# Seams between the stages of an encoder block: a wider first group, other block sizes, u copied in portions, squares summed by TensorE

## The chip, the core and the metric

The kernel runs on one core of one Trainium2 chip. A core has TensorE (PE; its weight loads are PEld), VectorE (DVE), ScalarE (ACT), GpSimd (POOL) and SyncE (SP, which here only issues DMAs). The metric is the device time of one execution in microseconds (us), as the median of several runs. 512 frames of 1024 channels go through one layer.

## What is computed

The reference, cut to what matters (all in float32):

```python
mod = (silu(c) @ w_ada + b_ada).reshape(B, 3, 3, 1024)
h = modulate(rms_norm(x, g_ffn1), mod[:, 0, 0], mod[:, 0, 1])
x = x + 0.5 * mod[:, 0, 2] * swiglu(h, w_ffn1_in, w_ffn1_out)

h = modulate(rms_norm(x, g_mix), mod[:, 1, 0], mod[:, 1, 1])
u_pool, u_ssm, gl_pool, gl_ssm = split(h @ w_in)
y_pool = multiscale_pool(u_pool, pool_w, pool_b, pool_scale) @ w_pool_up
y_ssm = s5_mixer(u_ssm, ...) @ w_ssm_up
x = x + mod[:, 1, 2] * ((sigmoid(gl_pool) * y_pool + sigmoid(gl_ssm) * y_ssm) @ w_out)

h = modulate(rms_norm(x, g_ffn2), mod[:, 2, 0], mod[:, 2, 1])
x = x + 0.5 * mod[:, 2, 2] * swiglu(h, w_ffn2_in, w_ffn2_out)
return rms_norm(x, g_final)
```

`swiglu` is `(silu(h @ Wa) * (h @ Wb)) @ Wout` with 2816 = 22 x 128 inner channels; a "tile" f below is one of these 22. The S5 mixer needs small tables (angles, powers, sines) that are computed from parameters.

## The kernel before, in words

**Arithmetic.** Frames lie along the free dimension, 128 channels on the partitions. A product is exact enough in three matmuls (`mm3`, L255-L258): every weight tile `raw` is split into a high part `wh` (a cast by ScalarE, L1295) and a low part `wl = raw - wh` (L1297, VectorE, or GpSimd if the unit has `pool_lo`); activations are split likewise into HH and HL, or GHA and GLA (`put_split`, L260-L262; `gslots` also has a slot pair in GC).

**Units.** The program is a list `units`, walked once in order. A unit with weights has its raw tile loaded by a DMA and split some units ahead (`split_at`, `load_at`, L1261-L1270: about two units of lead for the split, three buffers), then issues its matmuls (`mm`) and what follows from them (`post`). All engines take their instructions strictly in the order written. So an instruction of VectorE that waits holds up the splits written behind it, and through them TensorE.

**First feed-forward.** `group6` (L271) runs over the 8 chunks k of the input channels: per k it makes h (L215, L219, L246) and 18 matmuls of 512 columns for six output halves at once (three tiles f, with a and b). In this first group VectorE also computes the modulation `mod`: each k needs two dots of 1024 columns (L132), whose weights come by DMA. Then each further tile takes two in-units of 24 matmuls (ab = 0, 1), after the second of which `gate_store` (L399) forms silu(a) * b. After the tiles of a block (BLOCKS, L19: 6, 6, 5, 5 tiles) 8 out-units, one for each output chunk d, of 3 matmuls per tile, add to the residual (`residual`, L646). The unit loop's end (L1374-L1385) gives VectorE further work by the unit's index: one more dot from unit 16 on (`ada_step`), and from 18 on up to ten small operations for the SSM tables (`fill`, L707 in the profile).

**Seams.** The last two output chunks of each stage are done in `tail` (L330) by halves of the frames, HA and HB, so that the sum of squares of the next norm can start: squares by ScalarE (L185, L348), added into ACC by GpSimd (L186) or VectorE (L349), summed over the channels by TensorE with a column of ones (`norm_sum`, L192), then a root, a reciprocal and a matmul that spreads it over the partitions (`norm_rows`, L206).

**Mixer.** A `group6`, then 18 units of 24 matmuls for u, the gates and the rest. The group's four tiles of u_ssm are copied from PSUM to U in 16 pieces of 32 x 128 each (`ssm_u`, L992), before TensorE's `ssm_in` can use them; VectorE then does pool sums (L1075-L1085), complex products (L705) and scans (L1026).

**Second feed-forward.** `ffn_seven` (L447) computes the tiles 4 to 21 in pairs with seven products in the place of eight, in halves of 256 frames (`half_units`, matmuls at L492). Their operands are sums of h (`h_sums`, GpSimd, from float32 copies HF that GpSimd makes at L221) and of weights (GpSimd, L510-L512), split late (`late_splits`). The end is a tail, and eight products of `final` (L660) with their output DMAs.

## Time and profile before

| | |
|---|---|
| median of 3 runs | 1063.01 us (1061.71 to 1063.97) |
| the profiled execution | 1061.94 us, its span 1059.9 us |
| TensorE busy | 1025.5 us (97%) |
| VectorE busy | 750.5 us (71%) |
| ScalarE, GpSimd busy | 377.6, 405.7 us |
| HBM read | 134 MB, 130 GB/s over the span |

TensorE is nearly always busy, so its idle time, some 34 us, and the parts of the span where its granted clock (PEclk) is under 1.00 are all that another order could win. In the profile's rows an entry "[3.23 <-DVE wl L1297]" says that the engine sat idle for 3.23 us before the instruction until VectorE had written wl at line 1297. Names without a number are buffers; "x32" is a count. A row of a window gives, for each engine, busy time and instructions, then PEclk, the DMA engines' share and GB/s.

### The profile page before, as it was taken

To read this page: it belongs to the slowest core of one execution; us is meant where nothing else is said; L and a number is where in the kernel's file an instruction comes from. 1 tells how busy PE (TensorE), PEld (TensorE's weight loads), DVE (VectorE), ACT (ScalarE), POOL (GpSimd) and SP (SyncE) were. 2 spreads that over 40 slices of the span, in tenths; PEclk is the share of its full clock that TensorE was granted. 3 is DMA by queue.
4 is the path that set the end of the run, shared out by engine and by line. 5 is a ranking of instruction groups with operands and counts; after the bars stand their busy time and mean duration, and the time that the engine had idled before them with its cause. 6 is when DMAs were issued, how large, how long until landed. Compare 5 with 4: busy or idle time off the path is not lost.

```text
span 1059.9 us, 14235 instructions
## 1 busy us (share of the span) xinstructions
PE 1025.5 (97%) x5474; PEld 870.2 (82%) x5474; DVE 750.5 (71%) x1152; ACT 377.6 (36%) x546; POOL 405.7 (38%) x339
## 2 busy tenths in 40 slices
PE   7899999999999999989999999999999999999996
PEld 6678888888888888877888888887888998999895
DVE  6966888999796546689922365377984995798454
ACT  5242222222232243453243333235442442343244
POOL 2310200389885513044600000298762571475003
PEclk8999999999999999999999999999999999999998
DMA  9555555464566122412234223231351242235102
GB/s 347 213 198 181 198 200 189 171 227 166 176 243 219 58 76 76 130 40 90 92 102 145 80 100 100 60 117 63 100 179 40 100 157 63 80 106 173 61 20 80
DMA packets 45893, 138.22 MB, mean 130 GB/s; under 512 B 5105, under 2 KB 9329, under 8 KB 45826
## 3 DMA queue, kind: packets, MB, share of 16 engines
q1 hardware_dynamic: 45650, 136.73, 38.1%
q8 instruction: 43, 0.70, 0.3%
q0 software_dynamic: 176, 0.59, 0.1%
q14 instruction: 24, 0.20, 0.1%
HBM read 134.15 MB, written 3.15 MB: 130 GB/s over the span
## 4 chain that ended last, share of the span: by engine, by line
PE 82%; DVE 11%; POOL 2%; issue 1%; ACT 1%; DMA 1%; SPq 0%; DVEq 0%; ACTq 0%; POOLq 0%
PE ps L256 20%; PE ps L258 20%; PE ps L257 20%; PE ps L492 16%; PE ps L281 1%; PE ps L282 1%; DVE ev L705 1%; PE ps L285 1%; DVE U L997 1%; DVE ev L215 1%; DVE QM L132 1%; DVE TB L132 1%; DVE ACC L349 1%; DVE wl L1297 1%; PE ps L942 1%
## 5 line engine op out<-in xcount | busy, mean ns | idle before, releaser
L1297 DVE TENSOR_TENSOR wl<-raw,wh 128x1024 fp32r<-128x1024 f32 (+3 forms) x150 | 186.0, 1244 | 78.3 <-ACT wh L1295 78.1
L1295 ACT CAST wh<-raw 128x1024 fp32r<-128x1024 f32 (+3 forms) x164 | 150.4, 922 | 185.5 <-PE ps L257 99.9
L258 PE MATMUL ps<-HH,wl 128*128 128x512 f32 (+1 forms) x544 | 212.0, 390 | 4.6 <-DVE wl L1297 4.6
L256 PE MATMUL ps<-HH,wh 128*128 128x512 f32 (+1 forms) x544 | 212.6, 391 | 0.0
L257 PE MATMUL ps<-HL,wh 128*128 128x512 f32 (+1 forms) x544 | 211.7, 389 | 0.0
L258 PEld LDWEIGHTS ps<-HH,wl 128*128 128x128 f32 x544 | 102.3, 188 | 29.0 <-DVE wl L1297 5.4
L256 PEld LDWEIGHTS ps<-HH,wh 128*128 128x128 f32 x544 | 102.4, 188 | 23.4 <-ACT PM L938 0.2
L257 PEld LDWEIGHTS ps<-HL,wh 128*128 128x128 f32 x544 | 102.5, 188 | 23.3
L256 PE MATMUL ps<-GHA,wh 128*128 128x512 f32 (+1 forms) x308 | 118.8, 386 | 0.0
L258 PE MATMUL ps<-GHA,wl 128*128 128x512 f32 (+1 forms) x308 | 118.0, 383 | 0.0
L257 PE MATMUL ps<-GLA,wh 128*128 128x512 f32 (+1 forms) x308 | 117.9, 383 | 0.0
L186 POOL TENSOR_TENSOR ACC<-ACC,ev 128x512 f32<-128x512 f32 x15 | 19.4, 1296 | 246.8 <-ACT ev L185 246.7
L646 DVE SCALAR_TENSOR_TENSOR X<-ps,MOD,X 128x512 f32<-128x512 f32 (+1 forms) x78 | 55.0, 706 | 73.9 <-PE ps L258 73.9
L132 DVE CUSTOM_DVE_ANT_0 ADA<-ADA,C,COL 128x1024 f32<-128x1024 f32 x50 | 74.8, 1496 | 0.0
L256 PEld LDWEIGHTS ps<-GHA,wh 128*128 128x128 f32 x308 | 57.8, 188 | 12.7 <-ACT PM L938 0.4
L258 PEld LDWEIGHTS ps<-GHA,wl 128*128 128x128 f32 x308 | 57.8, 188 | 12.7
L257 PEld LDWEIGHTS ps<-GLA,wh 128*128 128x128 f32 x308 | 57.8, 188 | 12.3
L281 PE MATMUL ps<-HH,wh 128*128 128x512 f32 (+1 forms) x180 | 61.6, 358 | 6.0 <-ACT HH L219 5.9
L492 PE MATMUL ps<-SH,wl 128*128 128x256 f32 x216 | 61.0, 282 | 0.0
L282 PE MATMUL ps<-HH,wl 128*128 128x512 f32 (+1 forms) x180 | 60.3, 350 | 0.5 <-DVE wl L1297 0.5
L492 PE MATMUL ps<-SL,wh 128*128 128x256 f32 x216 | 60.7, 281 | 0.0
L492 PE MATMUL ps<-SH,wh 128*128 128x256 f32 x216 | 60.7, 281 | 0.0
(253 smaller groups left out, 2158.1 us busy)
## 6 DMA issues: line engine op xcount, KB each, us to landing
ADA<-w_ada SPq DMA_DIRECT2D x50, 512.0 KB, 3.6
raw<-w_f_in SPq DMA_DIRECT2D x40, 512.0 KB, 4.6
raw<-w_f_out SPq DMA_DIRECT2D x40, 384.0 KB, 4.1
raw<-w_in SPq DMA_DIRECT2D x18, 512.0 KB, 3.5
MISC<-w_f_in SPq DMA_DIRECT2D x18, 512.0 KB, 3.5
raw<-w_f SPq DMA_DIRECT2D x16, 384.0 KB, 3.9
raw<-w_f_out SPq DMA_DIRECT2D x16, 320.0 KB, 3.0
MM<-w_f_in SPq DMA_DIRECT2D x9, 512.0 KB, 3.6
```

The lines of the kernel that those rows point to most:

```text
L132: V.tensor_tensor_reduce(out=t, in0=t, in1=C, scale=1.0, scalar=bada[:, n:n + 1], op0=ALU.mult, op1=ALU.add, accum_out=MOD[:, n:n + 1],)
L186: eng.tensor_tensor(out=acc[:, cs], in0=acc[:, cs], in1=sq[:, cs], op=ALU.add)
L215: V.scalar_tensor_tensor(out=t[:, cs], in0=X[:, k, cs], scalar=GS[:, s * 8 + k:s * 8 + k + 1], in1=r[:, cs], op0=ALU.mult, op1=ALU.mult,)
L256: E.matmul(pst, wh, xh, start=first, stop=False)
L257: E.matmul(pst, wh, xl, start=False, stop=False)
L258: E.matmul(pst, wl, xh, start=False, stop=last)
L281: E.matmul(pst[m][:, cs], hi[:, w], xh, start=first, stop=False)
L282: E.matmul(pst[m][:, cs], lo[:, w], xh, start=False, stop=False)
L492: E.matmul(out_, w_[:, i, w], x_, start=first and n == 0, stop=last and n == 2, skip_group_check=True)
L646: V.scalar_tensor_tensor(out=X[:, d, cs], in0=p[:, cs], scalar=MOD[:, s * 24 + 16 + d:s * 24 + 17 + d], in1=X[:, d, cs], op0=ALU.mult, op1 ...
L1295: S.copy(out=hi[:, 0:u.cols], in_=t)
L1297: eng.tensor_tensor(out=lo[:, 0:u.cols], in0=t, in1=hi[:, 0:u.cols].bitcast(F32), op=ALU.subtract)
```

## The change

It has six parts.

1. The first feed-forward's group takes seven halves per k (three tiles and the a-half of a fourth; 896 columns), and the in-unit of that half goes. The low parts there are made by VectorE, each one unit ahead, and by GpSimd no longer; the first loads of weights are issued together. GpSimd's first instruction is now the load of the SSM tables.
2. BLOCKS becomes 5, 5, 6, 6. With the missing unit, the unit's index at which dots and small operations are handed out meets other units.
3. At the seams the last squares are not added by VectorE. `norm_sum` runs over several terms and lets TensorE add them. `prefetch` (splits and loads) comes later in the tail of stages 0 and 1, and at stages 1 and 2 the group's first two low parts are VectorE's, the third GpSimd's.
4. The four tiles of u are copied after the group, after each of the two u-units, and after the first gate unit (`gp`, m = 6). Within a tile the copying engine changes with t, not with m.
5. In the second feed-forward ScalarE makes the copies HF. After tile 3 come eight out-units of 4 tiles, the first four with one late split each, and then the pairs, with out-units of 6 tiles behind every third pair; a slot is found by `slot_of`. The last block has 6 tiles.
6. At the end GpSimd does one of the four last products of `final`.

```diff
-BLOCKS = ((0, 6), (6, 12), (12, 17), (17, 22))
+BLOCKS = ((0, 5), (5, 10), (10, 16), (16, 22))
...
-    def norm_sum(pc, cs=ALL):
+    def norm_sum(pc, cs=ALL, more=()):
...
-        for b in range(b0, b1):
-            E.matmul(pc[:, b:b + 1], ACC[:, b * P:(b + 1) * P], ONE[:, 0:1], start=True, stop=True)
+        terms = [ACC] + list(more)
+        for n, x in enumerate(terms):
+            for b in range(b0, b1):
+                E.matmul(pc[:, b:b + 1], x[:, b * P:(b + 1) * P], ONE[:, 0:1], start=n == 0 and b == b0,
+                         stop=n == len(terms) - 1, skip_group_check=True)
...
         if s == 2:
-            G.tensor_scalar(out=HF[k % 4][:, cs], in0=t[:, cs], scalar1=shift_col(s, k), scalar2=None, op0=ALU.add)
+            S.activation(out=HF[k % 4][:, cs], in_=t[:, cs], func=AF.Identity, bias=shift_col(s, k))
...
-            u = Unit(src[k], 768, mm, pre, (lambda: post(pst)) if k == KT - 1 else None)
-            u.pool_lo = pre0 is not None or k < 3
+            u = Unit(src[k], nm * P, mm, pre, (lambda: post(pst)) if k == KT - 1 else None)
+            u.pool_lo = pre0 is None and k == 2
...
-            rc = norm_sum(nrm["pc"], HA)
-            add6 = first(6, p6, HB)
+            rc = norm_sum(nrm["pc"], HA, [sq7])
+            sq6 = first(6, p6, HB)
...
-            prefetch()
-            add7 = first(7, p7, HB)
-            add6()
-            add7()
+            nrm["sq"] = [sq6, first(7, p7, HB)]
             if s < 2:
+                prefetch()
                 make_h(s + 1, 1, nrm["A"])
             else:
-                rc = norm_sum(nrm["pc"], HB)
+                rc = norm_sum(nrm["pc"], HB, nrm["sq"])
...
-                if m % 2:
+                if t % 2:
                     V.tensor_copy(out=o, in_=i)
                 else:
                     S.copy(out=o, in_=i)
...
-            for m in range(4):
-                ssm_u(m, pst[m])
+            held.extend(pst[0:4])
+            ssm_u(0, held[0])
...
+            return std_unit(wi[m], HH, HL, 8, lambda h: (pool_in(1 - m, h[0]), ssm_u(1 + m, held[1 + m])))
...
+                if m == 6:
+                    ssm_u(3, held[3])
...
+        n = len(units)
+        out_units(0, 4)
+        for u in units[n:n + 4]:
+            u.pre = lambda: late_splits.pop(0)()
...
+            if i in (6, 12):
+                out_units(i - 2, i + 4)
...
+        if j < KT:
+            split_at[j] = j - 1
...
+    rb = ev()
+    S.copy(out=rb[:, HB], in_=nrm["B"][0][:, HB])
+    final(0, 2, (rb, HB), G)
+    for k in range(2, KT, 2):
```

What this does to the order of VectorE's instructions at three places. First, one k of the first group (PM, QM and TB hold weights of the dots). Before:

```order
L215 SCALAR_TENSOR_TENSOR ev<-X,GS,ps 128x512
L132 ISA QM,MOD<-QM,C,COL 128x1024
L132 ISA MOD 128x1
L141 SCALAR_TENSOR_TENSOR GS<-MOD,COL 128x1
L246 SCALAR_TENSOR_TENSOR HL<-ev,MOD,HH 128x512
L132 ISA QM,MOD<-QM,C,COL 128x1024
```

After (the lines have moved by 3):

```order
L218 SCALAR_TENSOR_TENSOR ev<-X,GS,ps 128x512
L132 ISA QM,MOD<-QM,C,COL 128x1024
L132 ISA MOD 128x1
L141 SCALAR_TENSOR_TENSOR GS<-MOD,COL 128x1
L249 SCALAR_TENSOR_TENSOR HL<-ev,MOD,HH 128x512
L132 ISA QM,MOD<-QM,C,COL 128x1024
L132 ISA MOD 128x1
L1309 TENSOR_TENSOR wl<-raw,wh 128x896
```

VectorE's split of the weights has come to the end of each k. Second, the small operations of unit 30 (PM holds the tables in the making). Before, in an in-unit of block 2, between the splits of two units of 1024 columns:

```order
L1297 TENSOR_TENSOR wl<-raw,wh 128x1024
L132 ISA ADA,MOD<-ADA,C,COL 128x1024
L132 ISA MOD 128x1
L707 TENSOR_TENSOR PM<-PM 128x112
L707 TENSOR_SCALAR PM<-PM 128x112
L707 SCALAR_TENSOR_TENSOR PM<-PM 128x112 x5
L707 TENSOR_SCALAR PM<-PM 128x112
L707 SCALAR_TENSOR_TENSOR PM<-PM 128x112 x2
L1297 TENSOR_TENSOR wl<-raw,wh 128x1024
```

After, in an out-unit of block 2 (640 columns):

```order
L1309 TENSOR_TENSOR wl<-raw,wh 128x640
L651 SCALAR_TENSOR_TENSOR X<-ps,MOD,X 128x512
L132 ISA ADA,MOD<-ADA,C,COL 128x1024
L132 ISA MOD 128x1
L712 TENSOR_TENSOR PM<-PM 128x112
L712 TENSOR_SCALAR PM<-PM 128x112
L712 SCALAR_TENSOR_TENSOR PM<-PM 128x112 x5
L712 TENSOR_SCALAR PM<-PM 128x112
L712 SCALAR_TENSOR_TENSOR PM<-PM 128x112 x2
L1309 TENSOR_TENSOR wl<-raw,wh 128x640
```

The same ten operations now stand between the splits of shorter units, with a residual beside them. Third, VectorE's copies of u behind the mixer's group, with buffer numbers and the engines waited for. Before:

```order
L1085 TENSOR_TENSOR MISC_87<-MISC_87,FIX_93 128x4x4 [waits DMASW1_49,DVE_49]
L997 COPY U_3519<-ps_3203 32x128 [waits PE_49]
L997 COPY U_3519<-ps_3203 32x128 x15
L997 COPY U_3519<-ps_3205 32x128 [waits PE_49]
L997 COPY U_3519<-ps_3205 32x128 x15
L1297 TENSOR_TENSOR wl_3612<-raw_3475,wh_3611 128x1024 [waits DMAHW3_49,Activation_49]
```

After:

```order
L1090 TENSOR_TENSOR MISC_87<-MISC_87,FIX_93 128x4x4 [waits DMASW1_49,DVE_49]
L1002 COPY U_3522<-ps_3201 32x128 [waits PE_49,Activation_49]
L1002 COPY U_3522<-ps_3201 32x128 [waits Activation_49] x7
L1309 TENSOR_TENSOR wl_3567<-raw_3478,wh_3566 128x1024 [waits DMAHW2_49,Activation_49]
L1002 COPY U_3522<-ps_3202 32x128 [waits PE_49,Activation_49]
L1002 COPY U_3522<-ps_3202 32x128 [waits Activation_49] x7
```

There are eight copies of a tile on VectorE, not sixteen of two tiles, a split stands between two portions, and each copy waits for ScalarE; ScalarE's copies wait for VectorE in the same way.

## The prediction

> **What bounds the kernel now.** I read the page first, then the list of TensorE's waits, then the timelines of VectorE, ScalarE and TensorE at each of those waits, and windows of the stretches around them. The page says who is the bound:

> ```profile
> PE 1025.5 (97%) x5474; PEld 870.2 (82%) x5474; DVE 750.5 (71%) x1152; ACT 377.6 (36%) x546; POOL 405.7 (38%) x339
> ```

> TensorE is busy for 1025.5 of 1059.9 us, and the change leaves its large matmuls alone in number. So only TensorE's idle time and its low clock can be won, and any new wait of TensorE is lost in full. Where the idle time is, the waits of TensorE tell (columns: who waits for whom, us in total, times, longest):

> ```profile
> PE ps L281 <- ACT HH L219: 5.9, 7, 1.1
> PE ps L196 <- DVE ACC L349: 5.8, 5, 2.9
> PE ps L258 <- DVE wl L1297: 4.6, 2, 3.2
> PE ps L492 <- DVE wl L262: 3.1, 3, 1.4
> PE ps L206 <- DVE rc L200: 1.6, 2, 1.1
> PE ps L492 <- ACT wh L261: 1.3, 2, 1.1
> ```

> Every row is a seam: the first group (L281), the sums of squares between stages and at the end (L196, L206), the mixer's start (L258), the start of the second feed-forward's pair units (L492). The change works on all of these. VectorE has 29% of idle time overall, but it does not lie in the stretches where the change adds work, and that decides the sum.

> One pace is needed throughout. In the window 100 to 112 TensorE has no gap:

> ```profile
> 100.00:112.00 12.00, 12.00 (x53) 9.69 (x52) 8.54 (x16) 2.00 (x4) 0.00 (x0) 1.00 0.67 230
> ```

> Its 53 matmuls include some two cut by the edges, so a 512-column matmul takes about 0.233 us: a group unit of 6 tiles (18) 4.2, of 7 tiles (21) 4.9, an in-unit (24) 5.6, an out-unit of 5 tiles (15) 3.5.

> **The change part by part: the first group.** VectorE's and GpSimd's rows of one period:

> ```profile
> 28.01 0.74 DVE L215 SCALAR_TENSOR_TENSOR ev<-X,GS,ps 128x512 f32<-128x512 f32 x1
> 28.67 1.27 DVE L132 CUSTOM_DVE_ANT_0 QM<-QM,C,COL 128x1024 f32<-128x1024 f32 x1
> ...
> 30.06 0.74 DVE L246 SCALAR_TENSOR_TENSOR HL<-ev,MOD,HH 128x512 fp32r<-128x512 f32 x1
> 30.72 2.87 DVE L132 CUSTOM_DVE_ANT_0 QM<-QM,C,COL 128x1024 f32<-128x1024 f32 x1
> ...
> 33.53 0.73 DVE L215 SCALAR_TENSOR_TENSOR ev<-X,GS,ps 128x512 f32<-128x512 f32 x1
> ```
> ```profile
> 30.31 2.21 POOL L1297 TENSOR_TENSOR wl<-raw,wh 128x768 fp32r<-128x768 f32 x1 [3.31 <-ACT wh L1295]
> ```

> The split that VectorE does elsewhere, for 1024 and 768 columns:

> ```profile
> 178.88 1.22 DVE L1297 TENSOR_TENSOR wl<-raw,wh 128x1024 fp32r<-128x1024 f32 x1
> ...
> 201.12 0.95 DVE L1297 TENSOR_TENSOR wl<-raw,wh 128x768 fp32r<-128x768 f32 x1
> ```

> The period is 33.53 - 28.01 = 5.52 us against TensorE's 4.2, which makes the 1.1 us waits of L281. The second dot takes 2.87 instead of 1.27 because GpSimd's split runs beside it. After the change VectorE does the split itself: 5.52 - 1.60 + about 1.05 (896 columns, between 0.95 and 1.22) = 4.97, against 4.90 on TensorE for seven tiles. The group so takes the seventh tile, 24 x 0.233 = 5.6 us of later work, almost free: 7 periods of 5.52 become 7 of 4.97 (-3.9), the later unit goes (-5.6), the last run grows (+0.7), and unit 1 now waits for its split in VectorE's queue (+1 to +3). Sum -4.8, ends -3 and -7. GpSimd's queue now begins with the load of the SSM tables (576 KB), some 48 us earlier than now, amid the loads of the first tiles. I cost it at nothing, since the dots at 28.67 and 30.72 start with no idle time ahead, their tiles being there; uncovered it is rival four.

> **Blocks of 5, 5, 6, 6.** The small SSM operations are handed out ten to a unit, by the unit's index, whatever the unit's length. In before the heavy ones fall on in-units of 5.6 us. Now block 2's out-units, 3.5 us each, get them. The windows hold those of the units 29 to 34, VectorE's L707 only (length, busy):

> ```profile
> 176.85:178.90 2.05, 1.84 (x10) 1.00 0.44 140
> 181.27:184.00 2.73, 2.46 (x10) 1.00 0.56 183
> 188.32:190.93 2.61, 2.34 (x10) 1.00 0.52 165
> 193.02:195.30 2.28, 1.99 (x10) 1.00 0.48 156
> 199.36:201.15 1.79, 1.58 (x10) 1.00 0.46 98
> 203.90:205.53 1.63, 1.53 (x10) 1.00 0.37 68
> ```

> The other work of an out-unit on VectorE, and of the gate before it:

> ```profile
> 173.61 0.69 DVE L403 TENSOR_TENSOR ev<-ev,ps 128x512 f32<-128x512 f32 x1 [1.07 <-PE ps L258]
> 174.98 0.69 DVE L262 TENSOR_TENSOR GLA<-ev,GHA 128x512 fp32r<-128x512 f32 x1 [0.69 <-ACT GHA L261]
> ...
> 201.99 0.74 DVE L646 SCALAR_TENSOR_TENSOR X<-ps,MOD,X 128x512 f32<-128x512 f32 x1
> 202.65 1.27 DVE L132 CUSTOM_DVE_ANT_0 ADA<-ADA,C,COL 128x1024 f32<-128x1024 f32 x1
> ```

> From start to start a residual is 0.66 and a dot with its read 1.28; a split of 640 columns is about 0.74. So an out-unit holds VectorE for 0.74 + 0.66 + 1.28 = 2.7 plus its small operations of 2.0, 2.7, 2.6, 2.2, 1.7, 1.6: in sum 29.0 us, while TensorE needs 6 x 3.5 = 21.0. Count from the end of unit 28, where the gate (2.0, idle included), a dot and some 1.5 of small ones come first: the split for unit 31 is ready at 5.7, needed at 7.5; that for 32 at 10.4, needed at 11.0. Then splits are late: 33 by 1.4, 34 by 1.8, 35 by 1.4, 36 by 1.0, 37 by 1.2. That is 6.8 us of new waits, each too short to lower the clock; 0.2 more for a fuller stretch behind. **+7.0**, ends +4 (another unit of lead) and +9.

> **The seams of squares.** Behind the first feed-forward and the mixer the adds of L349 leave VectorE and TensorE sums the tiles itself. The rows for the end show the wait and what stands in it:

> ```profile
> 1045.93 0.58 PE L196 MATMUL ps<-ONE,ACC 128*128 128x1 f32 x4 [0.23 <-DVE ACC L349]
> 1051.34 0.61 PE L196 MATMUL ps<-ONE,ACC 128*128 128x1 f32 x4 [2.85 <-DVE ACC L349]
> ```
> ```profile
> 1049.55 1.73 DVE L349 TENSOR_TENSOR ACC<-ACC,ev 128x256 f32<-128x256 f32 x1 [0.21 <-ACT ev L348]
> ...
> 1053.76 2.48 DVE L663 TENSOR_TENSOR MISC<-X,ps 128x512 f32<-128x512 f32 x4 [1.32 <-PE ps L206]
> ```
> Of the 5.8 us in the list, 0.23 + 2.85 are these two; 2.7 are the inner seams, three waits of 0.9. They go, but each inner seam gets 6 more matmuls of one column. Two of them (four records) take 0.58, so one costs 0.2 to 0.3: 12 cost 2.4 to 3.6, of which two of a seam's six run while TensorE waits for the last square anyway. Net **-0.3 at each inner seam** (-1.3 to +0.5). At the end the first sum costs 0.2 more than its wait. The second then waits only for the last square, which is there when the add of it starts, at 1049.55: 1051.34 becomes 1049.6 (-1.7). Three finals instead of four stand on VectorE (2.48 / 4 = -0.6), and GpSimd does the fourth beside them. **-2.0** (-1 to -3).

> **The mixer's start.** The copies of u, all 32 x 128, and the waits behind them:

> ```profile
> 453.81 9.60 DVE L997 COPY U<-ps 32x128 f32<-32x128 f32 x32
> ...
> 463.44 1.23 DVE L1297 TENSOR_TENSOR wl<-raw,wh 128x1024 fp32r<-128x1024 f32 x1
> ```
> ```profile
> 448.80 8.63 ACT L999 COPY U<-ps 32x128 f32<-32x128 f32 x32
> ```
> ```profile
> 464.72 0.67 PE L258 MATMUL ps<-HH,wl 128*128 128x512 f32 x1 [3.23 <-DVE wl L1297]
> 496.64 0.50 PE L258 MATMUL ps<-HH,wl 128*128 128x512 f32 x1 [1.34 <-DVE wl L1297]
> ```
> ```profile
> 464.70:467.50 2.80, 2.78 (x7) 2.21 (x8) 1.86 (x3) 2.05 (x3) 0.00 (x0) 0.53 0.50 171
> 467.50:470.00 2.50, 2.50 (x11) 1.99 (x10) 2.14 (x6) 0.29 (x1) 0.00 (x0) 0.84 0.32 104
> ```

> In before ScalarE copies m = 0 and 2 and VectorE m = 1 and 3, both at once. Now the engine changes with t, and in the order each copy waits for the one ahead of it on the other engine. A chain of 16 takes 8 x (0.27 + 0.30) = 4.6 us, 5.1 with 0.03 for each hand-over as an estimate, and VectorE can do nothing else in it. Four chains are 18.4 to 20.4 against 9.6: 9 to 11 us more on VectorE, between 448 and 511, where it has hardly a gap and twice makes TensorE wait. The portions help the first split: ready near 460.5 instead of 464.67, so the wait of 3.23 and its clock loss (2.8 x 0.47 + 2.5 x 0.16 = 1.7) go. They hurt the next four, each portion standing ahead of a split: 1.3, 3.7, 5.5 and 1 to 2 us of waits, and a clock drop behind the longest. That is +13 against -6.3: **+7**, ends +4 and +10.

> The clock is at 0.53 behind the wait of 3.23, so the new waits of 3.7 and 5.5 may each bring a drop; the sum takes one, and the second is in rival three. [...]

> The 16 copies of a chain read four groups of 32 partitions (b) of one bank of PSUM, and the order lets none of them overlap: 16 steps. [...]

> **The start of the second feed-forward.** TensorE's idle time, GpSimd's load and the clock there:

> ```profile
> 691.00:758.00 67.00, 60.74 (x347) 51.96 (x346) 50.71 (x65) 32.26 (x47) 54.63 (x51) 0.97 0.30 94
> 738.00:757.00 19.00, 15.04 (x101) 13.73 (x102) 17.88 (x18) 10.31 (x13) 11.31 (x8) 0.91 0.29 92
> ```

> In the second row TensorE idles 4.0 us and runs at 0.91 (another 15.04 x 0.09 = 1.4). The change puts eight out-units of 12 matmuls, 2.8 us each, ahead of the pairs, with one late split in each of the first four (2.5 us of VectorE in 2.8), and takes 16 copies from GpSimd. The pair units then have 22 us more of lead than now. I take 5.5 off, of the 6.0 that the list's L492 rows (3.1 + 1.3 + 0.2) and the clock hold: **-5.5**, ends -2 (half of them return at the first pair) and -6. The new slots and blocks behind it cost nothing: the last gate has 8 to 12 matmuls of the out-unit in front of its slot, as cover 2.0 to 2.8 us for a chain of L403 and L262 (2.0); without it, 0.5 each.

> **The sum**, on the profiled execution of 1061.94 us (span 1059.9): -4.8 + 7.0 - 0.3 + 7.0 - 0.3 - 5.5 - 2.0 = +1.1. This execution lies 1.07 under the median of 1063.01, so the median after is forecast as **1064.1**. A measurement of this kernel can tell 0.2%, 2.1 us, from no change.

> **Rivals.**
> 1. The copies do not hold VectorE (they pass each other, or ScalarE is late so that the splits come between). Then the mixer gains what its waits hold, about 4, instead of losing 7: 1053. For it: the portions do free the first split. Against it: the waits in the order. 12%.
> 2. The out-units' overload is covered, since the queue at 201 to 213 already runs near its limit without a wait: 7 less, 1057. Against it: 8 us of excess work. 20%.
> 3. Slower: a second clock drop (1.7) and the late splits of the mixer push the scans, which GpSimd's operations follow, another 2 us: 1068. [...] 20%.
> 4. The SSM load among the first tiles, in the stretch where the DMA engines are full (share 1.03, 416 GB/s):

> ```profile
> 15.00:20.00 5.00, 3.93 (x18) 3.63 (x18) 4.01 (x6) 1.50 (x2) 3.63 (x2) 0.50 1.03 416
> ```

> 0.59 MB more is 1.4 us there, and if the first two dots each wait for it, 3 us: 1067. 8%.

> The forecast itself gets 40%, its own range 1060 to 1068. The range 1056 to 1070 takes in two, three and four and leaves out the first. Faster by over 0.2% is 1060.9 and less: 8 of the forecast's 40, rival one, 19 of rival two: 0.39. Within: 17 of the forecast, 3 of the rest: 0.20. Slower, over 1065.1: 15, and rivals three and four but 2: 0.41.

> **What would show it.** Right: VectorE's period in the first group near 5.0; waits of TensorE for a split in five units near 180 to 200; waits before the gate units between 460 and 505; no wait at the first pairs; one gap near 1.1 at the end. Wrong: no TensorE wait in block 2's out-units, or copies of u on both engines that overlap. Either alone moves the sum by 7 or more.

## The result, and the profile after

The changed kernel takes 1076.24 us (median of 4 runs, 1075.60 to 1076.93) against 1062.36 us, a ratio of 1.0129 with a 95% interval of 1.0111 to 1.0147. It is 13.9 us slower; the forecast was 1064.1 with a range of 1056 to 1070. The profiled execution took 1076.93 us, with a span of 1074.9.

The engines' row of the page, and TensorE's six largest waits in the changed kernel (who waits for whom, us in total, times, longest). Line numbers have moved: L261, L259, L285, L284, L209 were L258, L256, L282, L281, L206:

```profile
PE 1036.9 (96%) x5528; PEld 877.2 (82%) x5528; DVE 732.7 (68%) x1156; ACT 384.7 (36%) x565; POOL 357.3 (33%) x312
```
```profile
PE ps L261 <- DVE wl L1309: 16.3, 12, 4.1
PE ps L259 <- ACT GHA L592: 3.8, 2, 2.8
PE ps L285 <- DVE wl L1309: 2.5, 2, 2.0
PE ps L209 <- DMA IDN<-ident: 1.9, 1, 1.9
PE ps L259 <- ACT wh L1307: 1.5, 2, 0.8
PE ps L260 <- DVE GLA L595: 1.2, 2, 1.0
```

The waits of before are gone or small: those of the first group (5.9 us), of the sums of squares (5.8) and of the pairs (4.4). In their place stand 16.3 us for splits by VectorE and 5.0 for the gate (L592, L595). (A wait of 4.0 us at the first sum, L196 for the ACC of L705, which the prediction's list of before leaves out, is gone too; one of 1.9 for the identity IDN stands near it.) Idle time as such hardly rose, from 34.4 to 38.0 us, and yet TensorE's busy time did by 11.4 us. Matmuls at half clock count as busy (2.80 of 2.80 us in the window from 487.50 below, at 0.50), the first matmul behind a wait is recorded with 0.50 us at full clock where the others have 0.40, and the sums over the channels have 36 more records; how the 11.4 us divide among these is not shown. The waits' places and the clock tell more than the sums. TensorE's waits at four stages, from its timeline:

```profile
28.05 0.50 PE L285 MATMUL ps<-HH,wl 128*128 128x512 f32 x1 [2.04 <-DVE wl L1309]
178.93 0.50 PE L261 MATMUL ps<-GHA,wl 128*128 128x512 f32 x1 [1.27 <-DVE wl L1309]
184.15 0.50 PE L261 MATMUL ps<-GHA,wl 128*128 128x512 f32 x1 [1.46 <-DVE wl L1309]
189.03 0.50 PE L261 MATMUL ps<-GHA,wl 128*128 128x512 f32 x1 [1.15 <-DVE wl L1309]
193.43 0.50 PE L261 MATMUL ps<-GHA,wl 128*128 128x512 f32 x1 [0.66 <-DVE wl L1309]
198.21 0.51 PE L261 MATMUL ps<-HH,wl 128*128 128x512 f32 x1 [1.03 <-DVE wl L1309]
...
484.68 0.80 PE L261 MATMUL ps<-HH,wl 128*128 128x512 f32 x1 [2.78 <-DVE wl L1309]
497.44 0.60 PE L261 MATMUL ps<-HH,wl 128*128 128x512 f32 x1 [4.10 <-DVE wl L1309]
...
845.94 0.79 PE L259 MATMUL ps<-GHA,wh 128*128 128x512 f32 x1 [2.76 <-ACT GHA L592]
847.71 0.80 PE L260 MATMUL ps<-GLA,wh 128*128 128x512 f32 x1 [0.98 <-DVE GLA L595]
```

Four stages show: the start (28.05), five units of block 2 (178 to 199), the mixer's start (484 to 498), and, where nothing was forecast, the first out-units behind the pairs (846). The clock behind the last two (length, then busy time of each engine, then PEclk):

```profile
484.70:487.50 2.80, 2.80 (x7) 2.23 (x8) 1.38 (x5) 1.12 (x5) 1.06 (x1) 0.50 0.53 174
487.50:490.30 2.80, 2.80 (x8) 2.23 (x7) 1.57 (x4) 1.00 (x4) 0.00 (x0) 0.50 0.03 13
...
845.95:848.75 2.80, 1.82 (x4) 1.12 (x5) 2.57 (x3) 0.67 (x1) 1.08 (x2) 0.50 0.00 0
848.75:851.55 2.80, 2.80 (x8) 2.22 (x7) 1.30 (x2) 0.83 (x1) 0.00 (x0) 0.50 0.00 0
```

Each of these two waits, of 2.78 and 2.76 us, was followed by 5.6 us at 0.50, which cost some 2.8 us more. Behind other waits the price was between nothing and 3.2 us, as the last section shows.

The new first group has the period that was forecast. One period of VectorE's queue there:

```profile
27.91 0.74 DVE L218 SCALAR_TENSOR_TENSOR ev<-X,GS,ps 128x512 f32<-128x512 f32 x1
...
30.63 1.28 DVE L132 CUSTOM_DVE_ANT_0 QM<-QM,C,COL 128x1024 f32<-128x1024 f32 x1
...
31.84 1.09 DVE L1309 TENSOR_TENSOR wl<-raw,wh 128x896 fp32r<-128x896 f32 x1
32.84 0.74 DVE L218 SCALAR_TENSOR_TENSOR ev<-X,GS,ps 128x512 f32<-128x512 f32 x1
```

The period is 32.84 - 27.91 = 4.93 us (forecast 4.97), and the second dot takes 1.28 in the place of 2.87.

The copies of u alternate as the order says. VectorE's rows, then ScalarE's between them:

```profile
458.51 0.28 DVE L1002 COPY U<-ps 32x128 f32<-32x128 f32 x1
459.11 0.28 DVE L1002 COPY U<-ps 32x128 f32<-32x128 f32 x1 [0.32 <-ACT U L1004]
```
```profile
458.83 0.25 ACT L1004 COPY U<-ps 32x128 f32<-32x128 f32 x1 [5.19 <-DVE U L1002]
```

A pair takes 0.60 us, two copies and two hand-overs of 0.03; a portion of 16 holds VectorE for 4.6 us, the four together 18.3, against 9.6 before.

And the place that was not foreseen. VectorE's queue before the wait at 845.94:

```profile
841.68 0.95 DVE L1309 TENSOR_TENSOR wl<-raw,wh 128x768 fp32r<-128x768 f32 x1
842.54 1.49 DVE L265 TENSOR_TENSOR HL<-MM,HH 128x768 fp32r<-128x768 f32 x1
843.96 1.27 DVE L586 TENSOR_TENSOR ev<-ev,ps 128x512 f32<-128x512 f32 x2
845.32 2.33 DVE L595 TENSOR_TENSOR GLA<-ev,GHA 128x512 fp32r<-128x512 f32 x2
```

TensorE finished the pair near 840.4 (12 matmuls of the first out-unit, 2.8 us, stand between that and the wait, which begins at 843.18). The gate's product (L586) stood 3.5 us further on in VectorE's queue, at 843.96: behind the rest of the pair's combination (to 841.68) and the two splits shown. From there it took 2.0 us more to the end of the wait, through ScalarE's cast (L592). So a cover of 2.8 us faced a queue of 3.5 and a chain of 2.0.

### The profile page after: what moved, and what is told of

Same layout as the page of the kernel before. It is cut to its first block, busy times and chain, and to the rows that moved or that the text cites. A ratio compares the mean times of both kernels' runs of the same rounds, so it can differ in the third digit from the quotient of the medians.

```text
span 1074.9 us, 14348 instructions
## 1 busy us (share of the span) xinstructions
PE 1036.9 (96%) x5528; PEld 877.2 (82%) x5528; DVE 732.7 (68%) x1156; ACT 384.7 (36%) x565; POOL 357.3 (33%) x312
## 4 chain that ended last, share of the span: by engine, by line
PE 79%; DVE 14%; ACT 3%; issue 2%; DMA 1%; SPq 0%; DVEq 0%; ACTq 0%
PE ps L261 18%; PE ps L259 18%; PE ps L260 18%; PE ps L490 16%; DVE wl L1309 3%; PE ps L285 2%; PE ps L284 2%; PE ps L288 2%; DVE ADA L132 2%; DVE PM L712 1%; DVE ev L710 1%; DVE U L1002 1%; DVE ev L218 1%; DMA IDN<-ident 1%; PE ps L947 1%
## 5 line engine op out<-in xcount | busy, mean ns | idle before, releaser
L1309 DVE TENSOR_TENSOR wl<-raw,wh 128x1024 fp32r<-128x1024 f32 (+4 forms) x164 | 191.2, 1169 | 92.4 <-ACT wh L1307 92.2
L261 PE MATMUL ps<-HH,wl 128*128 128x512 f32 (+1 forms) x536 | 210.7, 393 | 11.7 <-DVE wl L1309 11.7
L259 PE MATMUL ps<-HH,wh 128*128 128x512 f32 (+1 forms) x536 | 210.9, 393 | 1.5 <-ACT wh L1307 1.5
L1307 ACT CAST wh<-raw 128x1024 fp32r<-128x1024 f32 (+4 forms) x166 | 150.7, 913 | 168.2 <-PE ps L260 89.9
L260 PE MATMUL ps<-HL,wh 128*128 128x512 f32 (+1 forms) x536 | 209.5, 391 | 0.0
L261 PEld LDWEIGHTS ps<-HH,wl 128*128 128x128 f32 x536 | 101.6, 190 | 38.5 <-DVE wl L1309 15.2
L261 PE MATMUL ps<-GHA,wl 128*128 128x512 f32 (+1 forms) x308 | 118.9, 386 | 4.5 <-DVE wl L1309 4.5
L259 PE MATMUL ps<-GHA,wh 128*128 128x512 f32 (+1 forms) x308 | 119.4, 388 | 3.8 <-ACT GHA L592 3.8
L259 PEld LDWEIGHTS ps<-HH,wh 128*128 128x128 f32 x536 | 101.5, 189 | 25.2 <-ACT wh L1307 2.1
L186 POOL TENSOR_TENSOR ACC<-ACC,ev 128x512 f32<-128x512 f32 x15 | 19.4, 1293 | 223.2 <-ACT ev L185 223.2
L132 DVE CUSTOM_DVE_ANT_0 ADA<-ADA,C,COL 128x1024 f32<-128x1024 f32 x50 | 75.0, 1500 | 0.0
L261 PEld LDWEIGHTS ps<-GHA,wl 128*128 128x128 f32 x308 | 58.1, 188 | 18.7 <-DVE wl L1309 6.2
L259 PEld LDWEIGHTS ps<-GHA,wh 128*128 128x128 f32 x308 | 58.2, 189 | 17.1 <-ACT GHA L592 4.6
L285 PE MATMUL ps<-HH,wl 128*128 128x512 f32 (+1 forms) x188 | 63.8, 354 | 2.7 <-DVE wl L1309 2.5
L284 PE MATMUL ps<-HH,wh 128*128 128x512 f32 (+1 forms) x188 | 64.2, 356 | 1.2 <-ACT HH L222 1.0
```

Source lines behind the costliest of these rows:

```text
L132: V.tensor_tensor_reduce(out=t, in0=t, in1=C, scale=1.0, scalar=bada[:, n:n + 1], op0=ALU.mult, op1=ALU.add, accum_out=MOD[:, n:n + 1],)
L186: eng.tensor_tensor(out=acc[:, cs], in0=acc[:, cs], in1=sq[:, cs], op=ALU.add)
L259: E.matmul(pst, wh, xh, start=first, stop=False)
L260: E.matmul(pst, wh, xl, start=False, stop=False)
L261: E.matmul(pst, wl, xh, start=False, stop=last)
L284: E.matmul(pst[m][:, cs], hi[:, w], xh, start=first, stop=False)
```

## The experiments

All times are medians of 4 to 10 runs, beside runs of the kernel before taken together with them (medians 1062.37, 1062.73 and 1062.60). "After" is the changed kernel, 1076.24.

**The engine by m again, portions kept.** On after:

```diff
-                if t % 2:
+                if m % 2:
```

> The changed kernel, with the engine of the copies of u chosen by m again, the portions kept. Theory (alternation): the chains of alternating copies hold VectorE 4 x 4.9 = 19.4 us against 9.6 before, and that is most of the mixer's loss of 9.3 us; so VectorE is given back some 10 us, the waits of 2.78 and 4.10 us and their clock loss go, and the time falls by 6 to 9 us, to 1067 to 1070. Rival (portions): the place of the copies ahead of the splits is what costs, and the time falls by 2 us or less.

Measured: 1069.57 us, ratio to before 1.0074 (1.0049 to 1.0099), 6.7 less than after. The waits of 2.78 and 4.10 are gone, but the portion of m = 3 stands in one piece ahead of a split, and one wait of 5.11 is left:

```profile
476.65 1.34 DVE L1309 TENSOR_TENSOR wl<-raw,wh 128x1024 fp32r<-128x1024 f32 x1
477.92 4.79 DVE L1002 COPY U<-ps 32x128 f32<-32x128 f32 x16
...
489.65 1.22 DVE L1309 TENSOR_TENSOR wl<-raw,wh 128x1024 fp32r<-128x1024 f32 x1
```

The alternation is the larger cost; what is left comes from VectorE having copies at all in this stretch, as the run with all of them on ScalarE shows below.

**The alternation alone, on the kernel before.**

```diff
-                if m % 2:
+                if t % 2:
```

> The kernel before, with one thing changed: the engine of the copies of u goes by t, all copies still in one place. Theory (alternation): 64 copies in one chain of 0.3 us steps take 19.4 us in the place of 9.6 on VectorE; the wait of 3.23 us before the first gate unit grows to about 13, with a longer time at half clock: 1062.4 + 10 to 12 = 1072 to 1075. Rival (portions): the alternation is nearly free, 1062 to 1064.

Measured: 1072.78 us, 1.0100 (1.0080 to 1.0119), 10.4 us slower than before. One wait holds most of it, in TensorE's timeline; the wait of 3.23 that it grew from is part of it:

```profile
472.36 0.80 PE L256 MATMUL ps<-HH,wh 128*128 128x512 f32 x1 [12.03 <-ACT wh L1295]
```

It is ScalarE's cast that is late here, since ScalarE is in the chain as well. So the alternation costs 10 us with the copies in one place; the portions, which the change brought with it, hide some of that.

**All copies on ScalarE, portions kept.** On after:

```diff
-                if t % 2:
-                    V.tensor_copy(out=o, in_=i)
-                else:
-                    S.copy(out=o, in_=i)
+                S.copy(out=o, in_=i)
```

> The changed kernel with all copies of u on ScalarE, the portions kept. Theory (VectorE is what the mixer's start waits for): VectorE is rid of the copies altogether, 9.6 us more than with the engine by m, whose last portion still held a split up by 5.11 us; that wait and its half clock go too, another 3 to 6 us: 1064 to 1067. Rival (ScalarE's casts become late behind 16 copies of 0.27 us in a row): waits for wh take their place, 1069 to 1072.

Measured: 1065.61 us, 1.0026 (1.0016 to 1.0035), 10.6 less than after. In the mixer two waits are left, 0.48 and 2.15 us.

**The old blocks.** On after:

```diff
-BLOCKS = ((0, 5), (5, 10), (10, 16), (16, 22))
+BLOCKS = ((0, 6), (6, 12), (12, 17), (17, 22))
```

> The changed kernel with the old blocks of 6, 6, 5, 5 tiles in the first feed-forward. Theory (small operations on short units): the five waits between 178 and 199 (5.6 us of idle time) and the three between 232 and 247 (2.6) go, each with some 0.2 us of restart: 8 to 10 us less, 1066 to 1068. Rival (VectorE short of time wherever the small operations fall, since the group has taken a unit away): the waits move to other units, 0 to 3 us less.

Measured: 1067.99 us, 1.0049 (1.0033 to 1.0066), 8.3 less than after. Of the eight waits of the first feed-forward (8.2 us idle) one of 0.71 is left, at 221. 7.5 us of idle time went and 8.3 us were gained. The difference of 0.8 is no more than the runs spread (1065.4 to 1068.9), though 0.1 us for each wait would fit the 0.50 us of the first matmul behind it. The 0.2 us of restart for each wait in the expectation was the author's estimate; no run shows it.

**No small operations in the out-units.** On after:

```diff
-SMALL = 10
+SMALL = 12
-        if i >= 18 and i < n_ffn1 and fill:
+        if i >= 18 and i < n_ffn1 and fill and not 29 <= i < 37:
```

> The changed kernel, its blocks kept, with twelve small operations a unit, not ten, and none in units 29 to 36, the out-units of block 2. Theory (small operations on short units): the five waits between 178 and 199 go, 5.6 us of idle time and 1 of restarts; in-units of 5.6 us carry the rest: 6 to 9 us less, 1067 to 1070. Rival (VectorE's work as a whole is too much in this stretch): waits come back in units 37 to 50, 0 to 4 us less.

Measured: 1071.95 us, 1.0090 (1.0072 to 1.0108), 4.3 less than after: between the two expectations. All eight waits are gone, but a gate is late in the next block, with 3.19 and 0.73 us of wait and half clock behind it. VectorE's rows ahead of that gate say why:

```profile
257.08 2.92 DVE L132 CUSTOM_DVE_ANT_0 ADA<-ADA,C,COL 128x1024 f32<-128x1024 f32 x1
259.93 0.08 DVE L132 DVE_READ_ACCUMULATOR2_ANT MOD<- 128x1 f32 x1
259.93 2.65 DVE L1309 TENSOR_TENSOR wl<-raw,wh 128x768 fp32r<-128x768 f32 x1
262.50 0.67 DVE L403 TENSOR_TENSOR ev<-ev,ps 128x512 f32<-128x512 f32 x1
```

A dot of 2.92 and a split of 2.65, where 1.28 and 0.95 are usual: GpSimd makes the tables at this time (27.3 us busy in 28). GpSimd's step of 1024 columns (L903) starts at 248.78, in the changed kernel at 226.77: the tables came 22 us later and met a gate and the out-units behind it. L403, which reads ps, takes its usual 0.67 in the same stretch; why it is not slowed and the others are was not shown.

**The out-units of the second feed-forward half a pair later.** On after:

```diff
-            if i in (6, 12):
-                out_units(i - 2, i + 4)
+            if i in (7, 13):
+                out_units(i - 3, i + 3)
```

> The changed kernel with the out-units of the second feed-forward one pair half later (behind i = 7 and 13, not 6 and 12), so that one more pair half stands between the last gate and the matmuls that read it. Theory (late gate): the waits of 2.76, 0.98, 1.01 and 0.23 us go, and with them the half clock behind the first (3.3 us): 6 to 9 us less, 1067 to 1070. Rival (VectorE and GpSimd in each other's way, so that VectorE lags as a whole): the waits come back at the later place, 0 to 2 us less.

Measured: 1067.46 us, 1.0048 (1.0031 to 1.0065), 8.8 less than after. VectorE is as late as it was, the gate's product at nearly the same time:

```profile
842.61 1.27 DVE L586 TENSOR_TENSOR ev<-ev,ps 128x512 f32<-128x512 f32 x2
```

But TensorE has other products to do meanwhile and never waits there. So the lateness itself costs nothing here; only the place of the reader does.

**The last squares added by VectorE again.** On after, in all three tails:

```diff
-            rc = norm_sum(nrm["pc"], HA, [sq7])
+            tt_(ACC[:, HA], ACC[:, HA], sq7[:, HA], ALU.add)
+            rc = norm_sum(nrm["pc"], HA)
...
-            nrm["sq"] = [sq6, first(7, p7, HB)]
+            sq7 = first(7, p7, HB)
+            for q in (sq6, sq7):
+                tt_(ACC[:, HB], ACC[:, HB], q[:, HB], ALU.add)
+            nrm["sq"] = []
```

> The changed kernel with the last squares added by VectorE again, in all three places, and summed from ACC alone. Theory: at the two inner seams the sum by TensorE is worth about nothing (waits of 0.8 to 1.1 us against 12 records of one column); at the end VectorE's adds stand beside GpSimd's products and cost 1.7 us: 1 to 3 us slower than the changed kernel, 1077 to 1079. Rival (the end hangs on the output's DMAs, 1.8 MB at 340 GB/s): the same as the changed kernel within 0.7 us.

Measured: 1079.20 us, 1.0154 (1.0138 to 1.0170), 3.0 more than after. The two adds at the end (L714) take 3.79 us beside GpSimd's products, and the wait for them is the bulk:

```profile
1066.76 1.01 PE L198 MATMUL ps<-ONE,ACC 128*128 128x1 f32 x4 [4.28 <-DVE ACC L714]
```

It replaces one of 0.30. At the inner seams the next wait is 1.37 and 1.33 in the place of 0.45 and 0.42, about what the extra matmuls cost. So the sums by TensorE are a gain, and nearly all of it lies at the end. The rest of part 3, the later `prefetch` and the low parts of the groups, was not tried by itself.

**Part 1 alone, on the kernel before** (seven tiles, VectorE's splits, early loads; weights packed to fit).

```diff
-            u.pool_lo = pre0 is not None or k < 3
+            u.pool_lo = pre0 is None and k < 3
...
-        group6(s, w6, post6, pre0)
+        group6(s, w6, post6, pre0, 7)
...
-        split_at[j] = max(walls[-3] + 1, j - 4) if len(walls) >= 3 else j - SA
+        split_at[j] = max(walls[-3] + 1, j - 4) if len(walls) >= 3 else 0
+        if j < KT:
+            split_at[j] = j - 1
...
-            load_at[j] = max(split_at[j] - (3 if seconds else 2), back)
+            load_at[j] = max(split_at[j] - (3 if seconds else 2), back) if j > 3 else -1
```

> The kernel before with part 1 alone: seven tiles in the first group, VectorE's splits, the SSM tables loaded early. Theory: the changed kernel's first in-unit behind the group starts at 62.35 us, that of before, one unit further, at 67.04, and nothing later takes it back: 4 to 6 us less than before, 1057 to 1058.5. Rival (the small operations, a unit earlier in the program, make waits in the first feed-forward even with the old blocks): 1060 to 1063.

Measured: 1059.21 us, 0.9967 (0.9955 to 0.9979), 3.4 less than before. That is a gain, somewhat less than the 4 to 6 us expected. In the trace the mixer's first matmul comes 4.4 us earlier (411.16, not 415.53). Then the clock takes some back: behind the short waits of the seam (1.10, 0.84 and 0.33 us) it is granted 0.88, 0.50 and 0.77 in the three stretches of 2 us from 410, a loss of 1.7 us, while in the kernel before much the same waits (1.10, 0.83 and 0.33) left it at 1.00. The matmuls of 256 columns from 411.9 to 413.6 start 0.21 us apart, those of the kernel before 0.12. The mixer's wait of 3.23 then ends only 2.8 us earlier (461.90, not 464.72). The gain of the group is real by itself; how much of it reaches the end depends on that clock.

**Three corrections together**: copies on ScalarE, old blocks, later out-units. On after:

```diff
-BLOCKS = ((0, 5), (5, 10), (10, 16), (16, 22))
+BLOCKS = ((0, 6), (6, 12), (12, 17), (17, 22))
...
-            if i in (6, 12):
-                out_units(i - 2, i + 4)
+            if i in (7, 13):
+                out_units(i - 3, i + 3)
...
-                if t % 2:
-                    V.tensor_copy(out=o, in_=i)
-                else:
-                    S.copy(out=o, in_=i)
+                S.copy(out=o, in_=i)
```

> The changed kernel with three things together: copies of u all on ScalarE, the old blocks in the first feed-forward, the out-units of the second one half pair later. Theory (three separate causes in three places, all on TensorE's path): the gains add up, -8.3 and -8.8 as measured alone and 10 for the copies: 1076.2 - 27 = 1049, 13 us under the kernel before. Rival (one cause behind another, so that a wait taken away uncovers the next): 1053 to 1058.

Measured: 1046.75 us, 0.9849 (0.9834 to 0.9865): 29.5 less than after, where the single gains add to 27.7, and 2 us below what was expected. All of TensorE's waits of the run that exceed 0.4 us in total:

```profile
PE ps L261 <- DVE wl L1306: 3.3, 3, 2.2
PE ps L198 <- DVE ACC L710: 3.3, 1, 3.3
PE ps L209 <- DMA IDN<-ident: 2.0, 1, 2.0
PE ps L285 <- DVE wl L1306: 1.5, 2, 1.0
PE ps L284 <- ACT HH L222: 1.1, 3, 0.5
PE ps L1339 <- DVE ONE L111: 1.1, 1, 1.1
PE ps L209 <- DVE rc L203: 0.6, 1, 0.6
```

The wait at L198 is that of the first sum, 12.9 us into the program, not of the end. The gains add up, so the three causes are separate, and the change without these three things beats the kernel before by 1.5%.

**The same three, all copies in one place.** On the version of three:

```diff
-            held.extend(pst[0:4])
-            ssm_u(0, held[0])
+            for m in range(4):
+                ssm_u(m, pst[m])
...
-            return std_unit(wi[m], HH, HL, 8, lambda h: (pool_in(1 - m, h[0]), ssm_u(1 + m, held[1 + m])))
+            return std_unit(wi[m], HH, HL, 8, lambda h: pool_in(1 - m, h[0]))
...
-                if m == 6:
-                    ssm_u(3, held[3])
```

> The version of three (copies on ScalarE, old blocks, later out-units), but with all 64 copies at once behind the group. Theory (the portions are worth what keeps the casts in time): ScalarE is held 64 x 0.27 = 17 us, the casts for the first gate units wait behind it, and TensorE waits 6 to 10 us with half clock after: 1054 to 1058 against 1046.8. Rival (the split buffers cover it): 1047 to 1049.

Measured: 1054.56 us, 0.9932 (0.9916 to 0.9949), 7.8 more than with portions. TensorE waits once for a cast that stands behind the 64 copies:

```profile
461.84 0.80 PE L259 MATMUL ps<-HH,wh 128*128 128x512 f32 x1 [6.09 <-ACT wh L1302]
```

So the portions are worth 8 us where one engine copies.

**The same three, with the identity loaded first.** On the version of three:

```diff
+    nc.sync.dma_start(out=IDN, in_=a["ident"])
     ada_first(8)
     load(0)
     ada_first(0)
-    nc.sync.dma_start(out=IDN, in_=a["ident"])
```

> The version of three with the identity's 64 KB loaded ahead of the first weights. Theory: the wait of 1.98 us before the first spread matmul, for the DMA of IDN, goes, and the group starts earlier: 1 to 2 us less, 1045 to 1046. Rival (the DMA engines are full from 5 to 36 us, so the dots' tiles come as much later): 1046 to 1047.5.

Measured: 1046.14 us, 0.9853 (0.9836 to 0.9870): not to be told from the version of three. The wait for IDN went, and one for the first h came in its place:

```profile
19.94 0.59 PE L284 MATMUL ps<-HH,wh 128*128 128x512 f32 x1 [2.33 <-ACT HH L222]
```

The DMA engines are full in this stretch (share 1.01 to 1.04 between 10 and 36 us in the changed kernel), so what is loaded sooner can delay something else; which load came later was not traced.

## Why the prediction was wrong, point by point

The forecast was +1.1 us for the profiled execution; the spans differ by +15.0. Term by term, from landmarks in the traces: first the changed kernel against the kernel before, and, to part two terms that lie in one stretch, against the run with the old blocks and the run with the later out-units. The stretches follow each other without a gap, so the measured column adds up to the difference of the spans:

| term | forecast | measured | from |
|---|---|---|---|
| first group | -4.8 | -4.7 | b-half of the fourth tile at 62.35, not 67.04 |
| blocks and small operations | +7.0 | +8.9 | from there to the mixer's first matmul: 357.8 after, 348.8 with the old blocks |
| seam ahead of the mixer | -0.3 | +0.3 | the same stretch: 348.8 with the old blocks, 348.5 before |
| mixer, with the seam behind it | +6.7 | +9.3 | from 415.53 to 692.91 before, 420.12 to 706.78 after |
| group of the second feed-forward | 0 | +0.6 | from 692.91 to 705.00 before, 706.78 to 719.45 after |
| start of the pairs | -5.5 | -6.9 | from 705.00 to the last out-matmul's end at 1048.49 before, 718.74 to 1055.29 with the later out-units |
| out-units behind the pairs | 0 | +8.5 | from 719.45 to 1064.48 after, against the same run |
| end | -2.0 | -1.0 | from the last out-matmul to the end of the span, 11.4 before and 10.4 after |
| sum | +1.1 | +15.0 | |

The medians of the two runs give 8.3 for the blocks and 8.8 for the out-units.

**The step that failed** is the one in the part on the second feed-forward: "The new slots and blocks behind it cost nothing: the last gate has 8 to 12 matmuls of the out-unit in front of its slot, as cover 2.0 to 2.8 us for a chain of L403 and L262 (2.0); without it, 0.5 each." The chain was sized as if VectorE were free when the pair ends. It is not: the gate stands some 3.5 us deep in its queue, behind 1.3 us of the pair's combination and two splits that take 2.3. GpSimd's share in this is small: one of the two splits takes 1.49 us beside GpSimd's sums in the place of 0.95. In the kernel before, one more step of the loop over the pairs stood between gate and reader, as in the run with the later out-units, and nothing showed. The waits at the two places come to 5.0 us and the half clock behind the first, at 0.50 for 5.6 us, to some 2.8 more, of the 8.8 gained by moving the readers; 1.0 is not assigned. The price "without it, 0.5 each" was nearly nine times too small, since neither the queue nor the clock was in it. That term alone turns a forecast of 1064 into 1073, past the end of the range.

**Right in the mechanism, too small in size.** Blocks: waits of 1.4, 1.8, 1.4, 1.0 and 1.2 were forecast for the units 33 to 37, and 1.27, 1.46, 1.15, 0.66 and 1.03 came; the other 2.6 us (three waits at 233 to 247) were costed at 0.2. There GpSimd makes the tables, and VectorE's dots and splits take up to 3.42 and 2.92 us. Mixer: waits of 1.3, 3.7, 5.5 and 1 to 2 were forecast, and 1.36 (0.84 and 0.52), 0.67, 2.78, 4.10 and 0.71 came, less than in the sum; but the clock fell twice, not once (3.1 and 1.7 us lost to it, against 1.7 before), and the inner seams gave nothing back (12 extra records of one column at each, against waits of 0.8 to 1.1 us). Rival three had named a second drop, with a chance of 20%.

**Right.** The group's period (4.93 against 4.97); the pairs' start, where no wait is left and GpSimd is busy for 43% of the first 66 us and not for 82%; the alternation as a chain, which the run of it alone and the run without it both show.

**Right by luck: the size of the first group's term.** Its parts, -3.9, -5.6, +0.7 and 1 to 3, add up to -5.8 to -7.8 and not to -4.8; with them the forecast would have been near 1062. And the seven periods of before were not all 5.52 us long. TensorE's rows for the runs k = 3 and k = 7 of before:

```profile
35.07 0.51 PE L281 MATMUL ps<-HH,wh 128*128 128x512 f32 x1 [1.05 <-ACT HH L219]
...
57.14 0.50 PE L281 MATMUL ps<-HH,wh 128*128 128x512 f32 x1 [1.05 <-ACT HH L219]
```

The group's first matmul is at 20.72, so the first three periods took 14.35 us, 4.8 each, and all seven 36.4 and not 38.6. In the changed kernel they take 36.8, with the wait of 2.04 for unit 1's split in them. Two slips of about 2 us each cancel.

**The end.** The wait of 2.85 became 0.30, but only half of the forecast gain reached the end. Rows of VectorE and GpSimd:

```profile
1067.87 1.88 DVE L668 TENSOR_TENSOR MISC<-X,ps 128x512 f32<-128x512 f32 x3 [1.21 <-ACT ev L1401]
```
```profile
1064.68 4.79 POOL L668 TENSOR_TENSOR MISC<-X,ev 128x768 f32<-128x768 f32 x3 [7.17 <-ACT ev L377]
```

VectorE ends at 1069.75 and the span at 1074.9, 5.2 us later; before it was 1056.24 and 1059.9, 3.7 later. The 1.05 MB of HB take 3.2 us at the 330 GB/s seen from 1070 to 1073, where the DMA engines' share is 1.00. GpSimd's products of HA end only at 1068.2, so their output could be in the way of HB's. But in the run with the adds back they end at 1066.4, and the span still ends 5.4 us behind VectorE's last product (1071.88 and 1077.3). So why the end grew is open.

**Not tried.** A kernel that keeps the new blocks and moves GpSimd's tables apart from the gates, the drops of the clock, and parts 5 and 6 of the change by themselves.

## What to carry to other kernels

Before an operation is moved, ask what stands ahead of it in its engine's queue at that moment, not how long its own chain takes: cover has to pay for the queue too (3.5 us here, beside a chain of 2.0), and a reader put half a pair later gained 8.8 us without any faster chain. Handing work from engine to engine in small pieces made both of them wait for the whole chain (for the copies of u, 9.0 us of VectorE and 18.1 of ScalarE in the changed kernel); let one engine that has time do it all, in portions between the work that others wait for. Behind waits of 2.15 to 6.09 us the granted clock mostly fell, which cost 1.7 to 3.2 us more here and did not follow the wait's length; price it as a risk. And work that is dealt out by a unit's number has to be looked at again when the units' lengths change.

## What the runs showed of the hardware

```profile
488.30:491.10 2.80, 2.80 (x9) 2.20 (x10) 2.35 (x3) 0.62 (x1) 2.80 (x2) 0.67 0.59 186
491.10:493.90 2.80, 2.80 (x11) 2.21 (x10) 2.80 (x6) 2.32 (x4) 0.63 (x1) 0.72 0.54 189
```

What a wait cost in clock did not follow its length, and no length from which the clock falls is shown. Adding up what the windows behind a wait lack to 1.00, 3.1 us were lost behind the wait of 2.78, 1.7 behind that of 4.10, and 3.2 behind that of 6.09 in the run with all copies in one place (0.50, 0.50 and 0.87 in three windows of 2.80 us). The wait of 2.15 in the version of three cost 1.7; with the identity first the same wait of 2.15 cost nothing (the 512-column matmuls behind it start 0.23 us apart, the pace at a clock of 1.00), and nor did that of 2.04 at 28.05 (1.00 in the windows of 2 us behind it). Waits of 0.7 to 1.5 us in block 2 left the clock at 1.00, but the three short ones of the seam in the run of part 1 alone (1.10, 0.84 and 0.33 us) were followed by 0.50. A copy of 32 x 128 out of PSUM took 0.29 us on VectorE and 0.26 on ScalarE (medians of 32 each in the changed kernel), and a hand-over between them only 0.03: the alternation is costly because it is a chain, not because of the hand-overs.
